# A diffusion block kernel: the first five row blocks of two input projections summed without the token root, the shift added as column sums, modulation products in pairs

## The chip, the core and the metric

The kernel runs on one core of one Trainium2 chip. The core's engines are named as the profile names them: PE (TensorE) multiplies matrices, PEld is its loading of the stationary operand, DVE (VectorE), ACT (ScalarE) and POOL (GpSimd) work elementwise, and SP (SyncE) issues transfers. Sixteen DMA engines move data between HBM and the core's memory; transfers are asked for by SP, ACT and POOL, each through a queue of its own in which requests stand in order. Each engine carries out its instructions in the order of the built program and waits at an instruction until what it needs is there. The metric is the device time of one execution in microseconds (us), as the median of several runs.

## What is computed

A modulation vector made from `c` scales and shifts the normalised tokens; the result `h` goes through one wide input projection, which feeds attention, a Fourier mixer and gates. Cut to what matters here:

```python
shift, scale, gate = jnp.split(silu_c @ w_ada[l] + b_ada[l], 3, axis=-1)
h = _modulate(_rmsnorm(xs, norm_g[l]), shift[:, None], scale[:, None])
p = h @ w_l
...
y_b = (_fourier_mix(u_b) * jax.nn.silu(z_b)) @ w_pb

def _rmsnorm(x, g):
    xf = x.astype(jnp.float32)
    y = xf * lax.rsqrt(jnp.mean(xf * xf, axis=-1, keepdims=True) + EPS)
    return (y * g.astype(jnp.float32)).astype(x.dtype)
def _modulate(h, shift, scale):
    return h * (1 + scale) + shift
```

So for feature d and token t, h = x · rx(t) · gain(d) + shift(d), with gain(d) = norm_g(d) · (1 + scale(d)) and rx(t) the reciprocal root over all 2048 features of the token ("the root" below). There are 512 tokens, 2048 features and 256 context tokens.

## The kernel before

Features lie on the 128 partitions in 16 row blocks `kb` of 128, tokens along the free axis: `xt` is 128 x 16 x 512. The program has a first stage, which this change rewrites, and a long rest (products of `h` with the other weights, attention, branches, output), which it leaves as it is.

The first stage makes three things for each row block and uses them.

*Modulation* (`modulation`, `matvec`, `columns`, L462 and L534 to L591). For block kb the 256 columns of `w_ada` that give its shift and scale are loaded as two tiles `wa` of 1 MB. Sixteen small matmuls (L534, 32 output partitions x 256, in float32, two records each in the trace) multiply them with silu(c). The result is copied by ACT (`ado`, L542), turned by two transposes (L545), reduced by DVE (L551), and two DVE instructions make `shift` (L590) and `gain` (L591) of the block. Four `wa` tiles exist, so the weights of a block are asked for when the product two blocks earlier has ended. Blocks 0 to 2 are loaded through SP's queue, the others through POOL's.

*Rows* (`make_h`, L521 to L523). DVE multiplies `xt` by gain and root, ACT adds the shift and rounds to a high half `hhi`, DVE subtracts for a low half `hlo`. Ahead of the first block stand the token norms (`token_norms`, L482 to L503): all of `xt` is loaded first (L466, six loads), ACT and DVE square it, PE sums the squares over partitions (L497), ACT and DVE make the root (L501, L502), and four matmuls spread it over the partitions (`spread`, L508).

*Sums of u and z* (`start_work`, `mm3`, L328 to L330). Eight tiles of 128 output columns (t 0 to 3 are u, t 4 to 7 are z) are summed over all 16 row blocks, three matmuls for each tile and block (high x high, high x low, low x high), 384 in all, each 128 x 128 on 512 columns. Their weights come as pieces `wr` (L213, up to 512 KB), split into halves `whi` (ACT, L177) and `wlo` (DVE, L178). The u tiles stay in four PSUM banks ("pb" in the profile) through all blocks; z tiles go through two banks ("pc") and `keep` adds each to `part` in SBUF (L562, L564), so the third z tile of a block waits until the first is kept.

The order is left to a scheduler in this stage; the loop over `kb` asks for pieces, splits them (`SPLIT`) and hands out as much of the sums as the finished rows allow. Rows also feed `form_row` (L606 to L608) for later products. After the u sums follows the Fourier mixer: `halves` (L670, L671) makes sums and differences of u on DVE, splits them into `uh` and `ul`, the tables `fch` and `fsq` are split likewise, and PE multiplies (`channels`, then `positions`); the last 48 matmuls of the z sums stand beside this preparation. The first product of the rest (tile "x" in the profile) begins at 169.55 us.

## Time and profile before

| | us |
|---|---|
| median of 3 runs | 1306.72 (1304.67 to 1308.26) |
| the profiled execution, its own time | 1305.55 |
| its span, first to last instruction | 1303.3 |
| PE busy | 1279.5 |
| DVE busy | 995.1 |
| ACT busy | 685.4 |
| DMA moved | 318.54 MB, mean 244 GB/s |

The granted TensorE clock was 0.998 over the span. In the timeline a row gives start, duration, engine, line, operation, output<-input, and in brackets how long the engine had been idle and what ended that. Records of matmuls overlap, so the distance from one start to the next says more than a record's duration. In a row of windows each engine has its busy time and, as (x...), its number of records, then the granted clock, the busy share of the DMA engines and GB/s.

### The profile page before, as it was taken

How to read it: one execution, taken by the hardware profiler on the slowest of the kernel's cores; microseconds unless marked ns; L12 is line 12 of the kernel's file. 1: busy time of each engine (PE TensorE's matmuls, PEld its weight loads, DVE VectorE, ACT ScalarE, POOL GpSimd, SP SyncE). 2: the span in 40 equal slices, each digit the busy share in tenths (PEclk: the TensorE clock that was granted, in tenths of full speed). 3: DMA queues.
4: the chain of work that ended last, by engine and by line, in shares of the span. 5: the costliest groups of instructions: out<-in, count | busy, mean ns of one | idle time of the engine just before them, and what ended most of it. 6: DMA issues, size and time to landing. Idle time of an engine off the chain costs nothing.

```text
span 1303.3 us, 17544 instructions
## 1 busy us (share of the span) xinstructions
PE 1279.5 (98%) x6522; PEld 1047.4 (80%) x6522; DVE 995.1 (76%) x1295; ACT 685.4 (53%) x1079; POOL 180.6 (14%) x244
## 2 busy tenths in 40 slices
PE   6999999999999999999999999999999999999997
PEld 3577888888888888888888888888888888888885
DVE  4666899979688887657687766688798867887676
ACT  5222655555556465444254554666666646464544
POOL 0110011110202111011021010011110212221210
PEclk9999999999999999999999999999999999999999
DMA  9898487887899988976879897468872899998985
GB/s 382 338 373 349 178 244 183 242 243 255 209 284 260 265 287 271 292 209 179 273 200 267 294 224 258 169 221 245 251 230 82 236 246 250 244 212 232 220 205 173
DMA packets 103718, 318.54 MB, mean 244 GB/s; under 512 B 9808, under 2 KB 33104, under 8 KB 99280
## 3 DMA queue, kind: packets, MB, share of 16 engines
q0 software_dynamic: 30288, 123.75, 40.4%
q1 hardware_dynamic: 48720, 163.65, 35.3%
q10 hardware_dynamic: 24624, 30.02, 6.6%
q8 instruction: 51, 0.84, 0.2%
q14 instruction: 35, 0.29, 0.1%
HBM read 283.30 MB, written 34.09 MB: 244 GB/s over the span
## 4 chain that ended last, share of the span: by engine, by line
PE 91%; DMA 3%; DVE 2%; ACT 2%; issue 1%; SPq 0%; ACTq 0%; DVEq 0%
PE banks L328 10%; PE banks L329 10%; PE banks L330 10%; PE x L328 9%; PE x L330 9%; PE x L329 9%; PE y L329 7%; PE y L328 7%; PE y L330 7%; PE pd L534 2%; PE banks L1294 2%; PE pb L328 2%; PE pb L330 2%; PE pb L329 2%; DMA wa<-in_w_ss 1%; PE pc L328 1%
## 5 line engine op out<-in xcount | busy, mean ns | idle before, releaser
L177 ACT ACTIVATE whi<-R 128x1024 fp32r<-128x1024 f32 x138 | 145.2, 1059 | 140.2 <-PE banks L330 47.3
L178 DVE TENSOR_TENSOR wlo<-R,whi 128x1024 fp32r<-128x1024 f32 x138 | 167.5, 1221 | 55.4 <-ACT whi L177 55.2
L178 DVE TENSOR_TENSOR wlo<-wr,whi 128x1024 fp32r<-128x1024 f32 (+1 forms) x123 | 148.5, 1212 | 63.4 <-ACT whi L177 63.2
L177 ACT ACTIVATE whi<-wr 128x1024 fp32r<-128x1024 f32 (+1 forms) x123 | 128.8, 1051 | 116.6 <-PE y L330 37.4
L328 PE MATMUL banks<-whi,s 128*128 128x512 f32 x396 | 157.1, 397 | 2.2 <-DVE ev L862 1.5
L330 PE MATMUL banks<-whi,s 128*128 128x512 f32 x396 | 155.2, 392 | 0.0
L329 PE MATMUL banks<-wlo,s 128*128 128x512 f32 x396 | 155.1, 392 | 0.0
L328 PE MATMUL x<-whi,s 128*128 128x512 f32 x352 | 137.2, 390 | 0.0
L330 PE MATMUL x<-whi,s 128*128 128x512 f32 x352 | 137.0, 389 | 0.0
L329 PE MATMUL x<-wlo,s 128*128 128x512 f32 x352 | 137.0, 389 | 0.0
L328 PE MATMUL y<-whi,s 128*128 128x512 f32 x316 | 123.1, 389 | 0.4 <-DVE cxe L1015 0.4
L329 PE MATMUL y<-wlo,s 128*128 128x512 f32 x316 | 123.1, 390 | 0.3 <-DVE wlo L178 0.3
L330 PE MATMUL y<-whi,s 128*128 128x512 f32 x316 | 122.8, 389 | 0.0
L281 POOL DMA_DIRECT2D R<-in_w_g x64 | 55.9, 874 | 420.2 <-DVE wlo L178 247.5
L177 ACT ACTIVATE s<-wr 128x512 fp32r<-128x512 f32 (+2 forms) x93 | 60.4, 676 | 68.6 <-DMA wr<-cf_d 21.8
L178 DVE TENSOR_TENSOR s<-wr,s 128x512 fp32r<-128x512 f32 (+2 forms) x93 | 66.8, 749 | 31.7 <-ACT s L177 30.9
L328 PEld LDWEIGHTS banks<-whi,s 128*128 128x128 f32 x396 | 74.4, 188 | 17.7 <-ACT whi L177 1.9
L330 PEld LDWEIGHTS banks<-whi,s 128*128 128x128 f32 x396 | 74.4, 188 | 15.5
L329 PEld LDWEIGHTS banks<-wlo,s 128*128 128x128 f32 x396 | 74.4, 188 | 14.0 <-DVE wlo L178 0.2
L330 PEld LDWEIGHTS x<-whi,s 128*128 128x128 f32 x352 | 66.1, 188 | 13.8
L329 PEld LDWEIGHTS x<-wlo,s 128*128 128x128 f32 x352 | 66.1, 188 | 13.6
L328 PEld LDWEIGHTS x<-whi,s 128*128 128x128 f32 x352 | 66.1, 188 | 13.6
(293 smaller groups left out, 2829.4 us busy)
## 6 DMA issues: line engine op xcount, KB each, us to landing
wr<-in_w_g SPq DMA_DIRECT2D x128, 512.0 KB, 5.2
R<-in_w_g POOLq DMA_DIRECT2D x64, 512.0 KB, 7.5
wa<-in_w_ss POOLq DMA_DIRECT2D x26, 1024.0 KB, 8.2
R<-in_w_g SPq DMA_DIRECT2D x32, 512.0 KB, 5.6
wr<-in_w_gate SPq DMA_DIRECT2D x32, 512.0 KB, 5.1
wr<-in_w_o SPq DMA_DIRECT2D x24, 512.0 KB, 7.7
R<-in_w_o POOLq DMA_DIRECT2D x24, 512.0 KB, 9.5
wr<-in_w_pab SPq DMA_DIRECT2D x20, 512.0 KB, 6.4
```

The source lines that it names most:

```text
L177: first = nc.scalar.activation(hi, src, ACT.Copy)
L178: return first, nc.vector.tensor_tensor(lo, src, hi.bitcast(F32), op=ALU.subtract)
L281: nc.gpsimd.dma_start(chain[e.pc], e.nxt, accum_op=ALU.add)
L328: nc.tensor.matmul(o, ah, bh, start=start, stop=False, skip_group_check=cont)
L329: nc.tensor.matmul(o, ah, bl, start=False, stop=False, skip_group_check=cont)
L330: nc.tensor.matmul(o, al, bh, start=False, stop=stop, skip_group_check=cont)
L534: last = nc.tensor.matmul(acc[32 * j : 32 * j + 32, :256], c2[:, 8 * h + k, :], w[:, k, :], start=n < 4, stop=n >= KK - 4)
L1294: nc.tensor.transpose(tp[:, k * P : (k + 1) * P], p[:, k * P : (k + 1) * P], ident)
```

## The change

The sums of u and z over the first five row blocks (`RAWS = 5`) are made from rows without root and without shift: `make_raw` gives ACT x · gain as the high half, and DVE the low half. For these blocks the u tiles are also taken out of PSUM into `part` after block 4. When the root is known, all eight kept sums are multiplied by it (`spread_rows`), and the sums go on with whole rows from block 5. The shift's part of the first five blocks is a product of one column with the weights: `shift_sums` multiplies four 256-column pieces of the raw weights with the block's shift (L574 of the changed file, float32, 32 output partitions), adds the results up over the blocks (`csum`), `shift_columns` turns them, and the last `keep` of each tile adds the column. Rows 0 to 4 are made once more with root and shift, for the later products.

The norms move behind the start: `squares` stands in the loop, DVE adds all 16 squares into one tile one after the other, and one matmul (`norm_sum`) and the spreading stand inside block 4. Loads on SP are put into one order by hand: weights of block 0, the first two blocks of x, pieces, weights of block 1, and so on, x in six chunks between; weights up to block 6 go through SP's queue. PE's order in the stage is written out by hand. From block 10 on the modulations come in pairs ahead of the rows that need them. Matmuls on constants (`warm`) stand ahead of the first modulation (7) and between it and the first sum (5). Modulations use two fixed PSUM tiles (`two`), in the second halves of which the column sums and the turned columns lie. The last pieces of the sums are cut anew: 36 matmuls of z, not 48, stand behind the last u matmul.

```diff
-STEPS = ([(0, 1, 0, 2), (0, 1, 2, 6)] + [(k, 1, 0, 8) for k in range(1, 4)]
-         + [(k, 2, t, 4) for k in range(4, 12, 2) for t in (0, 4)] + [(12, 2, 0, 4), (14, 2, 0, 4)]
-         + [(12, 4, t, 2) for t in (4, 6)])
+RAWS = 5
+STEPS = ([(0, 1, 0, 2), (0, 1, 2, 6)] + [(k, 1, 0, 8) for k in range(1, 6)]
+         + [(k, 2, t, 4) for k in range(6, 12, 2) for t in (0, 4)]
+         + [(12, 2, 0, 4), (12, 2, 4, 2), (14, 2, 0, 4), (14, 2, 4, 2), (12, 4, 6, 2)])
-XCH = [(0, 2), (2, 2), (4, 4), (8, 4), (12, 2), (14, 2)]
+XCH = [(0, 2), (2, 2), (4, 3), (7, 3), (10, 3), (13, 3)]
...
+    wada = {0: wada_load(0)}
+    load_x(0)
+    for _ in range(2):
+        load_start()
+    wada[1] = wada_load(1)
+    load_start()
+    load_x(1)
...
+    def squares(a, n):
+        for q in range(a, a + n):
+            v = sq[q // 2][:, q % 2, :]
+            nc.scalar.activation(v, xt[:, q, :], ACT.Square)
+            if q:
+                nc.vector.tensor_tensor(total, total, v, op=ALU.add)
+    two = [ps.tile([P, 512], F32, tag="b2", bufs=2, name=uid("pd")) for _ in range(2)]
+    cacc, wacc = two[0][:, 256:], two[1][:, 256:]
...
+    def shift_sums(kb):
+        w = [t[:, i : i + 256] for t, n in start_raw.pop(kb) for i in range(0, n, 256)]
+        for j in range(4):
+            nc.tensor.matmul(cacc[32 * j : 32 * j + 32], sf[:, kb, :], w[j], start=True, stop=True)
+        if kb == 0:
+            nc.scalar.copy(csum, cacc)
+        else:
+            nc.vector.tensor_tensor(csum, cacc, csum, op=ALU.add)
...
+    def norm_sum():
+        acc = bank3()
+        norm_acc.append(acc)
+        nc.tensor.matmul(acc, ones, total, start=True, stop=True)
...
+    def make_raw(kb):
+        rows_of(kb)
+        act = nc.scalar.activation(hhi[kb], xt[:, kb, :], ACT.Identity, scale=gain[:, kb, 0:1])
+        return nc.vector.scalar_tensor_tensor(hlo[kb], xt[:, kb, :], gain[:, kb, 0:1], hhi[kb].bitcast(F32),
+                                              op0=ALU.mult, op1=ALU.subtract), act
...
+    def keep(t, acc, kb, nk):
+        dst = pt(t)
+        if kb == 0 or t < 4 and kb < RAWS:
+            nc.scalar.copy(dst, acc)
+        elif kb + nk == KK:
+            nc.vector.scalar_tensor_tensor(dst, acc, corr[:, t : t + 1], dst, op0=ALU.add, op1=ALU.add)
+        else:
+            nc.vector.tensor_tensor(dst, acc, dst, op=ALU.add)
...
+    with tc.manual_schedule(engines={mybir.EngineType.PE}):
+        warm(7)
+        ins = modulate(0)
+        with behind((ins, columns(0))):
+            split_next()
+        warm(5)
+        for kb in range(RAWS):
+            ins = make_raw(kb)
+            with behind(ins):
+                for _ in range(2 if kb == 0 else 1):
+                    split_next()
+                if kb < RAWS - 1:
+                    squares(*XCH[kb])
+                if kb >= RAWS - 2:
+                    squares(*XCH[kb + 1])
...
+            if kb < RAWS - 1:
+                some((5, 3, 3, 3)[kb])
+            else:
+                some(2)
+                norm_sum()
+                some(1)
+            shift_sums(kb)
+            modulate(kb + 1)
+            some(1)
+            columns(kb + 1)
+            if kb == RAWS - 1:
+                act = norm_spread()
+            some(2 if kb == 0 else 4)
+            if kb + 2 <= RAWS:
+                load_start()
+        shift_columns()
...
+        ins = make_h(RAWS)
+        with behind(ins):
+            spread_rows(4, 5)
+            split_next()
...
+        for kb in range(6, KK, 2):
+            ins = make_h(kb), make_h(kb + 1)
...
+                some(8 if kb < KK - 4 else 4)
+                modulate(kb + 2)
+                modulate(kb + 3)
+                some(1 if kb < KK - 4 else 2)
+                columns(kb + 2)
+                columns(kb + 3)
```

`some(n)` is n tiles of the sums, three matmuls each; `modulate` is the product and the copy, `columns` the turning and what follows it.

339 lines of the change are left out of this document (191 added, 148 removed).

## The prediction

> **What bounds the kernel now.** I read the page first: the span, the busy times, the 40 slices, the chain that ended last.
>
> ```profile
> span 1303.3 us, 17544 instructions
> PE 1279.5 (98%) x6522; PEld 1047.4 (80%) x6522; DVE 995.1 (76%) x1295; ACT 685.4 (53%) x1079; POOL 180.6 (14%) x244
> ...
> PE   6999999999999999999999999999999999999997
> ...
> PE 91%; DMA 3%; DVE 2%; ACT 2%; issue 1%; SPq 0%; ACTq 0%; DVEq 0%
> ```
>
> PE is busy for 98% of the span and carries 91% of the chain; only the first of its slices, 32.6 us long, falls under 9. A gain must come from there, or from fewer matmuls. So I read the timeline of the first 30 us.
>
> ```profile
> 1.18 2.98 SPq L466 DMA_DIRECT2D xt<-in_xT  x6
> 4.20 0.95 SPq L462 DMA_DIRECT2D wa<-in_w_ss  x2
> 8.50 8.65 PE L497 MATMUL pd<-s,ones 128*128 128x512 f32 x16 [8.50 <-DVE s L496]
> 18.92 1.07 PE L534 MATMUL pd<-wa,c 128*32 128x256 f32 x16 [0.77 <-DMA wa<-in_w_ss]
> 20.06 0.37 ACT L542 COPY ado<-pd 128x256 f32<-128x256 f32 x1 [0.42 <-PE pd L534]
> 20.82 1.06 PE L508 MATMUL pc<-s 128*128 128x128 f32 x8
> 21.09 0.17 DVE L551 TENSOR_REDUCE adr<-pd 128x4 f32<-128x16 f32 x1 [0.99 <-PE pd L545]
> 21.71 1.46 PE L557 MATMUL pc<-ado,ones 128*128 128x256 f32 x6
> 21.91 0.75 DVE L521 SCALAR_TENSOR_TENSOR xt<-xt,gain,pc 128x512 f32<-128x512 f32 x1 [0.20 <-PE pc L508]
> 22.70 0.72 ACT L522 ACTIVATE s<-xt,shift 128x512 fp32r<-128x512 f32 x1 [0.16 <-DVE xt L521]
> 23.47 1.20 PE L328 MATMUL pb<-s,whi 128*128 128x512 f32 x4 [0.30 <-ACT s L522]
> ```
>
> The first sum starts at 23.47. Ahead of it stand the norms, which need all of x (six loads asked for from 1.18), and behind x in SP's queue the weights of modulation 0, whose second half is awaited until 18.92. From there copy, transposes, spreading of the root, DVE's row and ACT's row take 4.55 us. Then I asked how dense PE is afterwards, in two windows with the matmul groups of each (pb and pc on L328; L329 and L330 have the same counts).
>
> ```profile
> 23.47:63.01 39.54, 38.97 (x270) 23.38 (x271) 23.29 (x42) 10.16 (x17) 5.56 (x10) 1.00 0.91 357
> 63.01:141.27 78.26, 78.22 (x581) 55.64 (x581) 51.31 (x102) 23.92 (x35) 8.61 (x16) 1.00 0.85 330
> ...
> L534 PE MATMUL pd<-wa,c 128*32 128x256 f32 x161 | 12.9, 384 | 0.1
> L328 PE MATMUL pc<-s,whi 128*128 128x512 f32 x16 | 7.1, 446 | 0.1
> L328 PE MATMUL pb<-s,whi 128*128 128x512 f32 x17 | 6.6, 428 | 0.7 <-ACT s L522 0.7
> ...
> L328 PE MATMUL pb<-s,whi 128*128 128x512 f32 x47 | 18.9, 416 | 0.0
> L328 PE MATMUL pc<-s,whi 128*128 128x512 f32 x34 | 14.1, 414 | 0.0
> ```
>
> The chain of waits gives the price of each kind on PE, and one dense run the spacing of the sums.
>
> ```profile
> 62.69 0.23 PE pd L545 x2
> 78.13 1.86 PE pd L534 x32
> 79.99 0.43 PE pb L328
> ...
> 129.74 0.39 PE L328 MATMUL pb<-s,whi 128*128 128x512 f32 x1
> 132.24 0.39 PE L330 MATMUL pb<-s,wlo 128*128 128x512 f32 x1
> ```
>
> From 129.74 to 132.24 are eleven steps: 0.228 us a sum matmul. A modulation costs 1.86, 0.20 more on the matmul behind it (0.43 for 0.23), and 0.23 for its transposes: 2.29. The first window holds 99 sum matmuls and five modulations (161 records, 32 each): 22.6 + 11.4 = 34.0 of 39.54, so 5.5 us of waiting that the idle columns hardly name. The second holds 241 and ten: 54.9 + 22.9 = 77.8 of 78.26, so nothing to gain.
>
> **The start.** The new order loads the weights of modulation 0 first. The first x load (0.55 MB with the vectors) landed 3.9 us after 1.18, and the second half of those weights, 6.05 MB into the queue, at 18.92.
>
> ```profile
> xt<-in_xT SPq DMA_DIRECT2D x1, 512.0 KB, 3.9
> ```
>
> That is 13.8 us for 5.5 MB, 2.5 us a MB. At 2.05 MB the weights land at 5.1 + 3.75 = 8.85, and x at 10.1. From 18.92 to 23.47 were 4.55 us; DVE's multiplication (21.91 to 22.70) goes, so the row could be there at 12.6. But PE must first do five matmuls on constants, in a bank that DVE's reduction reads; it ended 2.34 us after the weights, and three such matmuls took 1.46 us, so five take 2.4: 8.85 + 2.34 + 2.4 = 13.6. Bounds: 12.6 if they cost nothing, 15.3 if PE is slow there (below). I take 13.6, a gain of 9.9.
>
> **Work added to PE behind the start.** Norm and spreading stood ahead of 23.47 and now stand inside block 4. A record of L497 took 0.43 in its dense part, as the weight loads show, and a matmul has two: 0.86, the spreading 1.06 (L508), and 0.20 each on the sum behind it. Shift sums: four matmuls shaped like L534, 8 of 32 records in 1.86, 0.47 a block, 2.3 for five; they stand beside a modulation, with no further change of kind. Turning their sum: 0.23. Modulations in pairs (blocks 10 to 15) save three changes, 0.6. Together +4.2. Bounds 3.6 (the shift sums run beside others at half their price, less the pairs) and 5.4 (each has a change of its own, 5 x 0.2, and pairs save nothing).
>
> ```profile
> 11.22 0.34 PEld L497 LDWEIGHTS pd<-s,ones 128*128 128x128 f32 x1 [0.52 <-DVE s L496]
> 12.27 0.19 PEld L497 LDWEIGHTS pd<-s,ones 128*128 128x128 f32 x1 [0.24 <-DVE s L493]
> 12.70 0.19 PEld L497 LDWEIGHTS pd<-s,ones 128*128 128x128 f32 x1 [0.24 <-issue]
> ```
>
> **Waits in the early blocks.** The order of the changed program is known, only its times are not. These rows carry the prices:
>
> ```profile
> L564 DVE TENSOR_TENSOR part<-pc,part 128x512 f32<-128x512 f32 x31 | 21.1, 686 | 5.0 <-PE pc L330 4.9
> L178 DVE TENSOR_TENSOR wlo<-wr,whi 128x1024 fp32r<-128x1024 f32 x15 | 18.2, 1220 | 1.0 <-ACT whi L177 1.0
> L523 DVE SCALAR_TENSOR_TENSOR s<-xt,shift,s 128x512 fp32r<-128x512 f32 x16 | 12.0, 749 | 3.2 <-ACT s L522 3.2
> L177 ACT ACTIVATE whi<-wr 128x1024 fp32r<-128x1024 f32 x15 | 15.6, 1047 | 1.2 <-DMA wr<-in_w_start 1.2
> ```
>
> I followed the engines block by block. (1) Blocks 0 and 1: the low half of the next row stands on DVE behind three `keep`: 0.4 and 0.9. (2) Modulations 2 and 4 write the PSUM tile whose other half DVE reads for the column sums: PE waits for an addition of 0.42 us (256 wide, as the row at 141.72 below) and in block 3 for the two DVE jobs ahead of it: 0.5 and 0.85. (3) In blocks 2 and 3 `keep` of the first z tile stands behind a weight split that starts after ACT's copy: 0.37 + 1.05 + 1.22 + 0.69 = 3.3 us, and PE has 0.68 + 0.23 + 1.37 = 2.3 us of other work until it needs that bank: 1.05 twice. (4) `norm_sum` waits for the last three of 15 additions in line on DVE, behind a `keep`: 0.69 + 3 x 0.69 less six matmuls, 1.4: 1.5. (5) Behind block 4 the low half of row 5 stands behind four `keep`, 1.05, and the root's copy keeps a bank, 0.5. Sum 7.8 against 5.5 now, so +2.3 if nothing overlaps better than counted, 0 if these waits are like today's, -2.8 if half of them vanish. I take +1.2.
>
> Hidden by DVE's idle time: 15 additions of squares (10.4), column sums (1.7), eight sums times the root (5.5), the low half of five rows a second time (3.7), 21 us in all. The two windows leave DVE idle for 16.25 and 26.95 us. In the early part, though, the additions, the column sums and four of the products, 14.9 us, meet 16.25: nearly full. Transfers: weights of blocks 3 to 6 move from POOL's queue to SP's, behind waits for PE; x and the pieces stand behind them. Weights of block 2 end 8.1 MB into the queue, 24.0 us by the rate above, and PE comes to them at about 25.3; later ones have more room. So loads cost nothing, and each us that they are late by more than 1.3 costs one.
>
> **The end of the stage.** Today ACT copies the u sums; now DVE does it, with the column, ahead of the table splits, and on ACT two splits of weights for the first product stand ahead of `uh`.
>
> ```profile
> 141.72 0.42 DVE L670 TENSOR_TENSOR u<-part 128x256 f32<-128x256 f32 x1
> 143.61 1.17 ACT L177 ACTIVATE uh<-u 128x512 fp32r<-128x512 f32 x2
> 144.12 1.22 DVE L178 TENSOR_TENSOR fsq<-wr,fsq 128x1024 fp32r<-128x1024 f32 x1
> 154.89 0.39 PE L328 MATMUL pb<-fsq,ah 128*128 128x256 f32 x1 [0.26 <-DVE al L178]
> ```
>
> Behind the last u matmul DVE has the last `keep` (0.85 with its handover), two table splits (1.22 each), one of a quarter (0.4) and two half-row jobs (0.7 in a row), then ACT `uh` (0.6): 5.0 us. PE has 12 matmuls, 2.7 us, and then stands before the Fourier matmuls: 2.3. Their low half stands behind two more jobs and a weight split on DVE: another 0.7. That is 3.0, against 0.26 idle ahead of 154.89 today. +2.7 if so, 0 if DVE gets there earlier; I take +1.8, nearer the upper end because the order of DVE is fixed there. The matmuls themselves are the same number. Behind this stage PE's order is the same, and PE was dense there.
>
> **Sum.** -9.9 + 4.2 + 1.2 + 1.8 = -2.7. The profiled execution of 1305.55 (its span 1303.3, and 2.25 around it) would become 1302.9; it stands 1.17 under the median of 1306.72, and from that the forecast is 1304.0.
>
> **Rivals.** *A second path, less waiting:* the early waits shrink to half of the list and the end costs nothing: -9.9 + 4.2 - 1.6 + 0 = -7.3, 1299.4; with today's waits and no cost at the end, -5.7, 1301.0. I give 1300.2. For it: from 63 us on PE never waited with DVE at 51.31 of 78.26. Against it: the program's order names the waits.
>
> *DVE becomes the bound (slower):* blocks 1 to 5, where 14.9 us of new DVE work meet 16.25 idle. If DVE falls behind, each late `keep` holds one of two banks and pushes the next; the list doubles to 15.6, that is 10.1 over today, and the end takes 2.7: -9.9 + 4.2 + 10.1 + 2.7 = +7.1, 1313.8; the middle of this case is 1310. It decides once the waits of these blocks pass 9.4 us (5.5 + 9.9 - 4.2 - 1.8). For it: the share; against it: from 145 to 150 us DVE is full and PE doesn't pause.
>
> ```profile
> 145.00:150.00 5.00, 5.00 (x24) 4.05 (x23) 5.00 (x12) 2.98 (x4) 0.00 (x0) 1.00 0.74 250
> ```
>
> *PE slow at the first sums:* weight loads took 0.34 until 11.22 and 0.19 from 12.27, with PE's first matmul at 8.50, so PE ran at about half rate for some 3.3 us. If the seven early matmuls on constants don't hold, or the holes behind them undo it, half of 3.3 us is lost, 1.7: 1305.7. Today's hole ahead of 18.92 (0.77) undid nothing. The Trainium skill, TensorE: Matmul & The Clock Gate, section "What's actually happening", says that PE's clock is halved by default, is released after about 3.4 us of sustained work and falls back after an idle window of that length; the trace agrees with the release (3.3 us). By that rule holes of 1 to 2 us, as here, would leave the clock up, and the sum stays as it is.
>
> *The change doesn't do what it says:* loads in flight share the engines, so that the first weights land with what was asked for beside them, 5.6 MB in, at 17.7: 22.5 instead of 13.6, +6.2, 1312.9. Against it: x landed piece after piece.
>
> **How the numbers follow.** Forecast 0.38, less waiting 0.32, DVE the bound 0.20, PE slow 0.06, loads together 0.04. About 0.3% (3.9 us) is what a measurement of this kernel can tell from no change: faster means under 1302.8, slower over 1310.6. The forecast's own range, by its bounds, is 1301 to 1307; a quarter of it lies under 1302.8. Faster: 0.10 + 0.31; slower: 0.12 from DVE, 0.03 from the loads; the rest 0.44. The range of 1298 to 1310.5 leaves out the far ends of the second and third case.
>
> **What would show it.** First sum (pb, L328) at 13.6: weights first. Modulation 6 begins with 123 sum matmuls done, by the sum at 13.6 + 28.0 + 5 x 2.29 + 4.8 + 6.7 = 64.6; near 61.8 it is less waiting, from 67.3 on the gain is gone, at 73.5 DVE is the bound. A wait of PE at `norm_sum` of about 1.5 on DVE, waits on pc for `keep`, and about 3 at the Fourier matmuls on ACT's `uh`: the single items. The window from modulation 6 to the last u matmul without waits. The forecast is wrong if the first sum starts after 15.5, or if a wait on a transfer of over 1 us stands between 14 and 66 us, or if PE loses time behind the stage, where its order hasn't changed.

## The result, and the profile after

The changed kernel is slower: 1314.49 us against 1306.12 us in the same comparison (medians of four runs each), a ratio of 1.0064 with a 95% interval of 1.0046 to 1.0081. The forecast was 1304.0 with a range of 1298 to 1310.5; the time lies outside it, on the other side. The profiled execution took 1313.97 us with a span of 1312.2, so 8.9 us of span have to be found. The page first: span, busy times, the slices of PE, the chain that ended last.

```profile
span 1312.2 us, 17694 instructions
PE 1281.3 (98%) x6568; PEld 1051.5 (80%) x6568; DVE 1011.6 (77%) x1328; ACT 691.6 (53%) x1095; POOL 176.3 (13%) x236
...
PE   8899999999999999999999999999999999999997
...
PE 86%; DMA 6%; DVE 5%; ACT 2%; issue 2%; SPq 0%; ACTq 0%; DVEq 0%
```

PE's busy time grew by 1.8 us only, and its share of the chain fell from 91% to 86%: most of the 8.9 must be waiting. In the slices of 33 us, where 699 stood now stands 889: the start is denser, and the second slice is no longer full. The timeline of PE around the first sum shows that the start did what was wanted.

```profile
10.50 0.44 PE L554 MATMUL pd<-ident,ado 128*128 128x128 f32 x2 [0.49 <-ACT ado L550]
11.21 2.43 PE L535 MATMUL pd<-s,ones 128*128 128x256 f32 x10 [0.27 <-DVE adr L560]
13.28 0.59 PE L328 MATMUL pb<-s,whi 128*128 128x512 f32 x1
```

The first sum starts at 13.28, 10.2 us ahead of today's 23.47. The windows behind it (busy time and records of each engine, then granted clock, DMA share, GB/s) show where this goes. The first two are cut where modulation 6 begins (70.10, with 123 sum matmuls done) and behind the last u matmul (146.12, with 348 done).

```profile
13.28:70.10 56.82, 47.94 (x348) 29.91 (x346) 36.64 (x65) 25.72 (x50) 1.26 (x2) 1.00 0.89 357
70.10:146.12 76.02, 74.56 (x567) 53.03 (x567) 59.70 (x123) 26.12 (x40) 8.64 (x16) 1.00 0.82 314
146.10:176.58 30.48, 27.54 (x182) 25.55 (x181) 29.42 (x46) 17.38 (x26) 0.54 (x1) 0.94 0.52 192
```

To modulation 6 the stretch is 17.3 us longer than the 39.54 of before. 24 more sums (123 for 99) are 5.5 of it, so 11.8 are new. The last window runs from 348 sums done to the first x product (176.58; before it is 169.39, not the 169.55 named ahead). The same stretch of the kernel before, where the 349th sum matmul starts at 143.31:

```profile
143.31:169.39 26.08, 25.82 (x182) 24.07 (x180) 25.29 (x38) 15.81 (x26) 0.54 (x1) 1.00 0.62 226
```

That is 4.4 us more. The account of the span: start -10.2, to modulation 6 +11.8, from there to 348 sums +1.2 (76.0 us for 225 sums, before 80.3 for 249, of which the 24 more are 5.5), the end of the stage +4.4, together +7.2 at the first x product; behind it 1135.6 us follow, 1133.9 before, +1.7. Of this, 0.4 stands in the last 10 us and came in every version of the changed kernel; the rest is within what executions differ by: over the profiled executions of this document the same rest took 1133.8 to 1139.9.

The single waits of the early blocks stand in the timeline; in brackets, PE's idle time and what ended it.

```profile
22.69 0.50 PE L329 MATMUL pb<-s,whi 128*128 128x512 f32 x1 [0.29 <-DVE s L611]
25.91 1.93 PE L541 MATMUL pd<-wa,c 128*32 128x256 f32 x32 [0.55 <-DVE csum L578]
28.87 1.06 ACT L177 ACTIVATE whi<-wr 128x1024 fp32r<-128x1024 f32 x1 [4.91 <-DMA wr<-in_w_start]
30.24 0.44 PE L554 MATMUL pd<-ident,ado 128*128 128x128 f32 x2 [1.50 <-ACT ado L550]
34.57 0.50 PE L329 MATMUL pb<-s,whi 128*128 128x512 f32 x1 [0.31 <-DVE s L611]
42.61 0.50 PE L328 MATMUL pc<-s,whi 128*128 128x512 f32 x1 [1.14 <-DVE part L639]
48.00 1.93 PE L541 MATMUL pd<-wa,c 128*32 128x256 f32 x32 [1.14 <-DVE csum L578]
53.50 0.50 PE L328 MATMUL pc<-s,whi 128*128 128x512 f32 x1 [1.08 <-DVE part L639]
58.15 1.13 PE L590 MATMUL pc<-s,ones 128*128 128x512 f32 x2 [1.65 <-DVE s L527]
66.33 0.50 PE L328 MATMUL pc<-s,whi 128*128 128x512 f32 x1 [0.42 <-DVE part L639]
68.62 0.50 PE L328 MATMUL pc<-s,whi 128*128 128x512 f32 x1 [0.41 <-ACT corr L583]
69.43 0.50 PE L329 MATMUL pc<-s,whi 128*128 128x512 f32 x1 [0.31 <-DVE s L620]
74.18 0.50 PE L328 MATMUL pc<-s,whi 128*128 128x512 f32 x1 [1.04 <-DVE part L639]
```

Most items that the prediction listed are there at nearly their size: column sums 0.55 and 1.14 (predicted 0.5 and 0.85), `keep` 1.14 and 1.08 (1.05 twice), `norm_sum` 1.65 (1.5). Smaller were the waits for the low halves of rows 1, 2 and 5: 0.29, 0.31 and 0.31 (0.4, 0.9 and 1.05). Two were not predicted, and in both a late transfer is behind it. ACT's copy of modulation 2 stood behind the split of a piece that landed only at 28.8; so PE, which had the modulation's transposes next, stood 1.50 us until 30.24. And 1.04 at 74.18: pieces asked for too late, as ACT's rows show (ACTq is its queue of requests).

```profile
64.30 0.59 ACT L600 COPY rx<-pc 128x512 f32<-128x512 f32 x1 [0.53 <-PE pc L599]
64.31 3.49 ACTq L213 DMA_DIRECT2D wr<-in_w_start  x2
67.84 0.72 ACT L619 ACTIVATE s<-xt,shift 128x512 fp32r<-128x512 f32 x1 [2.96 <-DVE part L639]
...
71.20 1.06 ACT L177 ACTIVATE whi<-wr 128x1024 fp32r<-128x1024 f32 x1 [2.58 <-DMA wr<-in_w_start]
```

The requests stand behind `rx` in ACT's order; they took 3.5 us, until 67.80, and ACT's row of block 5 came right behind them. (The profile names a DVE job as what ended that wait, but the DVE job that makes the row's input, L618, had ended at 65.67.)

At the end of the stage stands the wait that the prediction named, and DVE's line-up ahead of it: the last four `keep` of u, which ACT made before, two table splits, one quarter split, four sums and differences.

```profile
144.74 2.72 DVE L637 SCALAR_TENSOR_TENSOR part<-pb,corr,part 128x512 f32<-128x512 f32 x4
147.38 2.35 DVE L178 TENSOR_TENSOR fsq<-wr,fsq 128x1024 fp32r<-128x1024 f32 x2
149.65 0.41 DVE L178 TENSOR_TENSOR fch<-wr,fch 128x256 fp32r<-128x256 f32 x1
149.98 0.42 DVE L812 TENSOR_TENSOR u<-part 128x256 f32<-128x256 f32 x1
...
151.76 0.38 PE L328 MATMUL pb<-fch,uh 128*128 128x256 f32 x1 [2.77 <-ACT uh L177]
```

Behind the wait of 2.77 us the granted clock fell to half for one stretch of 3.4 us, as PE's windows show.

```profile
149.86:153.26 3.40, 1.33 (x9) 1.00 1.02 405
153.26:156.66 3.40, 3.40 (x16) 0.50 1.01 413
```

### The profile page after: what moved, and what is told of

The parts are those of the page before. It is cut to its first block, busy times and chain, and to the rows that moved or that the text cites. A ratio compares the mean times of both kernels' runs of the same rounds, so it can differ in the third digit from the quotient of the medians.

```text
span 1312.2 us, 17694 instructions
## 1 busy us (share of the span) xinstructions
PE 1281.3 (98%) x6568; PEld 1051.5 (80%) x6568; DVE 1011.6 (77%) x1328; ACT 691.6 (53%) x1095; POOL 176.3 (13%) x236
## 4 chain that ended last, share of the span: by engine, by line
PE 86%; DMA 6%; DVE 5%; ACT 2%; issue 2%; SPq 0%; ACTq 0%; DVEq 0%
PE banks L328 10%; PE banks L329 10%; PE banks L330 10%; PE x L330 8%; PE x L329 8%; PE x L328 8%; PE y L329 7%; PE y L328 7%; PE y L330 7%; DMA wr<-in_w_start 2%; PE banks L1436 2%; PE pd L541 1%; DMA wa<-in_w_ss 1%; DVE wlo L178 1%; PE pb L330 1%
## 5 line engine op out<-in xcount | busy, mean ns | idle before, releaser
L178 DVE TENSOR_TENSOR wlo<-wr,whi 128x1024 fp32r<-128x1024 f32 (+2 forms) x124 | 148.4, 1204 | 73.7 <-ACT whi L177 73.7
L177 ACT ACTIVATE whi<-wr 128x1024 fp32r<-128x1024 f32 (+2 forms) x124 | 128.7, 1044 | 130.9 <-PE banks L330 34.5
L330 PEld LDWEIGHTS x<-whi,s 128*128 128x128 f32 x352 | 66.1, 188 | 13.7
L328 PEld LDWEIGHTS x<-whi,s 128*128 128x128 f32 x352 | 66.1, 188 | 13.7
L329 PEld LDWEIGHTS x<-wlo,s 128*128 128x128 f32 x352 | 66.1, 188 | 13.6
```

The costliest lines, as they stand in the source:

```text
L177: first = nc.scalar.activation(hi, src, ACT.Copy)
L178: return first, nc.vector.tensor_tensor(lo, src, hi.bitcast(F32), op=ALU.subtract)
L328: nc.tensor.matmul(o, ah, bh, start=start, stop=False, skip_group_check=cont)
L329: nc.tensor.matmul(o, ah, bl, start=False, stop=False, skip_group_check=cont)
L330: nc.tensor.matmul(o, al, bh, start=False, stop=stop, skip_group_check=cont)
```

## The experiments

My theory A at the start: the loss is a handful of single waits, each made by one job that stands in a wrong place on DVE or ACT; each can be cured by a change of place. Rival B: DVE has too much to do in the early blocks and at the end; a cure in one place brings the wait back at the next. "x0" below is the start of the first x product in the profile: 169.4 before, 176.6 after. The ratios are to the kernel before, in the same comparison; those of single cures overlap with that of the changed kernel, so there the traces carry the reading. x0 is read from one execution: four executions whose code is the same that far had 348 sums done at 146.1 to 148.9, so 2 us of x0 alone show little. So "the end" is given too, the length of the stretch from 348 sums done to x0, in which the edits at the end of the stage act: 26.1 before, 30.5 after.

**The Fourier wait by order alone.** The sine tables are split behind the first half of u.

```diff
-    for q in range(2):
-        split_from(get(("dfts", q))..., fsq[:, 0, q], fsq[:, 1, q])
+    raws = [get(("dfts", q))... for q in range(2)]
     raw = get(("dftc", 0))
     split_from(raw, fch[:, 0, :], fch[:, 1, :])
-    for g in range(4):
-        halves(g)
+    halves(0)
+    halves(1)
+    for q in range(2):
+        split_from(raws[q], fsq[:, 0, q], fsq[:, 1, q])
+    for g in range(2, 4):
+        halves(g)
```

> The changed kernel with one thing moved: on DVE the table fch and the sums and differences of the first two u tiles stand ahead of the splits of the large table fsq (two of 1.22 us), and on ACT uh stands ahead of the second split of weights R. Theory A (the wait of 2.77 us ahead of the Fourier matmuls comes from what stands ahead of uh on DVE, and the granted clock of 0.5 behind it from the wait): the wait falls under 1 us, the clock stays at 1.0 up to 157 us, the 24 Fourier matmuls take about 3 us in place of 4.96, and the time falls by 3 to 5 us, to about 1310.5. Rival B (the first wait is only moved: ul, later splits or the loads of R take its place, and DVE is the bound in this stretch): under 1.5 us of gain, a wait of 1.5 us or more somewhere between 148 and 165 us.

Measured: 1317.83 us, ratio 1.0082 (1.0069 to 1.0095), x0 at 182.0, of which 2.8 us were lost ahead of the edit (348 sums were done at 148.9, against 146.1; behind a wait at 74.86 the clock fell). The end took 33.1 us, 2.6 more than in the changed kernel. The wait ahead of the Fourier matmuls was gone and a longer one stood behind them, where the z sums need a bank that DVE's `keep` (L637) frees:

```profile
159.76 0.79 PE L328 MATMUL pc<-s,whi 128*128 128x512 f32 x1 [3.90 <-DVE part L637]
```

B is right at the end of the stage. The windows above say why: there DVE is busy for 25.29 of 26.08 us in the kernel before and for 29.42 of 30.48 in the changed one. DVE has 4.1 us more to do in the stretch, and the stretch is 4.4 longer. It had hardly any reserve in the first place.

**The clock at the Fourier matmuls.** Twelve matmuls on constants fill the wait, so that PE does not pause.

```diff
             acc = bank()
+            for _ in range(12 if (g, m2) == (0, 0) else 0):
+                nc.tensor.matmul(acc[:, :P], ones, ones, start=True, stop=True)
```

> The changed kernel with 12 matmuls on constants (ones by ones, 128 columns, float32) in the wait ahead of the Fourier matmuls; nothing else is moved. They add no result. Theory A (PE's pause sets the clock back): the pause on PE shrinks to under 0.6 us, the granted clock stays at 1.0 between 153 and 157 us, the 24 Fourier matmuls take 3 to 3.3 us in place of 4.96 and the time falls by 1.5 to 2 us, to about 1312.7, although uh comes no earlier. Rival B (these matmuls are paced by ul and by the splits of ah, not by the clock): the 24 matmuls still take close to 5 us and the time stays at 1314.5 or rises by up to 0.5.

Measured: 1315.73 us, ratio 1.0074 (1.0059 to 1.0090), x0 at 176.9. The clock stayed at 1.00; 348 sums were done 1.2 us later than in the changed kernel, ahead of the edit, and the end took 29.6 us in place of 30.5. DVE was still the bound there: from 149.86 to 156.66 it was busy without a gap, and the z sums waited 0.42 for its `keep` at 156.94. Two versions below in which nothing is changed at the end and the clock happened to stay up (the column sums in the free tile, the additions on POOL) took 29.6 and 29.7 as well, with waits of 2.44 and 2.46 ahead of the Fourier matmuls. So the half clock at this place explains at most 0.8 of the 4.4 us.

**The column sums in the tile that is free.** They take the half of the PSUM tile that the next modulation does not write.

```diff
-    cacc, wacc = two[0][:, 256:], two[1][:, 256:]
+    wacc = two[1][:, 256:]
...
-        sp = two[kb % 2 if kb > 7 else 1][:, 256:]
+        sp = two[kb % 2][:, 256:]
...
+        cacc = two[kb % 2][:, 256:]
```

> The changed kernel with the column sums of each block put into the PSUM tile that the next modulation does not use. Theory A (the waits of PE ahead of modulations 2 and 4, 0.73 and 1.32 us, are those for DVE's addition in the other half of the same tile): both vanish; the first gives way to the wait on the copy of modulation 2, which stands behind a load, so 1.3 to 2 us are gained, time 1312.5 to 1313.2. Rival B (DVE is the bound in blocks 1 to 5): other waits of PE in 13 to 70 us grow by as much, and the time stays within 0.5 us of 1314.5.

Measured: 1315.42 us, ratio 1.0074 (1.0062 to 1.0086), x0 at 177.5. Both waits on `csum` went, and two on other jobs of DVE came: 1.84 on `keep` at 31.45 and 1.79 on a low half-row at 45.32, each with the half clock behind it. The scheduler had also changed DVE's order with the tile, so this run doesn't separate place from amount.

**Pieces asked for earlier, on SP.**

```diff
             if kb + 2 <= RAWS:
                 load_start()
+            if kb == RAWS - 2:
+                load_start()
+            if kb == RAWS - 1:
+                load_start()
         shift_columns()
         asks[0] = nc.scalar
-        ask_more(act, 2)
```

> The changed kernel with the next two pieces of weights asked for on SP's queue inside blocks 3 and 4, where ACT asked for them behind the copy of the spread root (64.3 us). Theory A (the transfers stood still between 56 and 62 us because nothing was asked for; the wait of 1.04 us at 74.18 on keep comes from the piece that landed late at 71.2, and row 5 on ACT stood 3 us behind its own requests at 64.3): the waits at 68.6 to 69.4 (0.7) and 74.18 (1.04) vanish, 1.2 to 2.2 us are gained, time about 1312.8. Rival B (DVE's additions are what PE waits for there, whatever the loads do): the wait at 74 stays over 0.8 us and the gain is under 0.6.

Measured: 1312.01 us, ratio 1.0047 (1.0035 to 1.0059), x0 at 174.7. The waits at 68.62, 69.43 and 74.18 were gone; modulation 6 began at 68.8 (70.1), and 348 sums were done at 144.3 (146.1). The late request cost about 2 us.

**Twelve of the fifteen additions of squares left out** (only squares 1, 8 and 15 are added to the first; the root is then that of four rows' squares).

```diff
-            if q:
+            if q in (1, 8, 15):
                 nc.vector.tensor_tensor(total, total, v, op=ALU.add)
```

> The changed kernel without 12 of the 15 additions of squares on DVE (8.3 us of its work between 14 and 58 us; the root is then made from four rows' squares only). DVE's other work keeps its order. Theory A (the waits of blocks 1 to 4 come from where a job stands in DVE's and ACT's order): the wait at norm_sum (1.65) and that of modulation 4 on the column sums (1.14), which stand behind such additions, go; the two of 1.14 and 1.08 on keep, which stand behind a weight split, and the one of 1.5 on the copy of modulation 2 stay. Gain 2.3 to 3 us, time 1311.5 to 1312.2. Rival B (DVE's amount of work is the bound in blocks 1 to 4): the keep waits shrink too, gain 5 us or more, under 1309.5.

Measured: 1312.86 us, ratio 1.0049 (1.0031 to 1.0067), x0 at 175.4; modulation 6 at 67.38, 2.7 earlier. DVE lost 12 jobs of 0.69, 8.3 us. `norm_sum` no longer waited; behind a wait at 72.10 the clock fell and took part of the gain again. The second `csum` wait halved to 0.55, but the waits for `keep` stayed as they were:

```profile
42.08 0.50 PE L328 MATMUL pc<-s,whi 128*128 128x512 f32 x1 [1.14 <-DVE part L639]
46.88 1.93 PE L541 MATMUL pd<-wa,c 128*32 128x256 f32 x32 [0.55 <-DVE csum L578]
52.38 0.50 PE L328 MATMUL pc<-s,whi 128*128 128x512 f32 x1 [1.06 <-DVE part L639]
```

So the two waits for `keep` don't come from the amount of work on DVE but from the job that stands ahead of the `keep`, the weight split behind ACT's copy. For them A is right; taking 8.3 us of work from DVE won 2.7 of the 8.8 us that PE waited up to modulation 6.

**The additions of squares on POOL.**

```diff
-                nc.vector.tensor_tensor(total, total, v, op=ALU.add)
+                nc.gpsimd.tensor_tensor(total, total, v, op=ALU.add)
```

> The changed kernel with the 15 additions of squares on POOL in place of DVE; the output is the reference's. Theory A: POOL is idle until 61.74 us and keeps up with the loads of x, so the same two waits go as without the additions, 2.3 to 3 us, time 1311.5 to 1312.2. Rival B (POOL takes over 2 us for an addition, or slows DVE's jobs down while both run): norm_sum waits for POOL longer than 1.65 us and nothing is gained, 1314 or more.

Measured: 1312.23 us, ratio 1.0048 (1.0032 to 1.0064), x0 at 174.9. It did about half of what leaving them out did: modulation 6 at 68.57, 1.5 earlier, the `keep` waits unchanged (1.14 and 1.05); `norm_sum` still waited 0.94, now for POOL, whose additions took 1.37 us in the mean, against 0.69 on DVE.

**The sine tables' low halves on POOL.**

```diff
-        split_from(get(("dfts", q))..., fsq[:, 0, q], fsq[:, 1, q])
+        raw = get(("dfts", q))...
+        nc.scalar.activation(fsq[:, 0, q], raw, ACT.Copy)
+        nc.gpsimd.tensor_tensor(fsq[:, 1, q], raw, fsq[:, 0, q].bitcast(F32), op=ALU.subtract)
```

> The changed kernel with the low halves of the table fsq (two of 1.22 us on DVE, ahead of u) made on POOL. Nothing is put later on DVE for it, unlike the version that only moved them behind u, which then waited 3.9 us for a keep of z. Theory A (the end of the stage is bound by the sum of DVE's work, which grew by the four keeps of u, 2.72 us): the wait ahead of the Fourier matmuls falls under 0.7 us and no wait over 1 us follows before 165 us, gain 2.4 to 4.5 us, time 1310 to 1312. Rival B (positions wait for POOL, or the loads of R bound the end): a wait over 2 us between 148 and 170 us, time 1313.5 or more.

Measured: 1312.28 us, ratio 1.0043 (1.0030 to 1.0056), x0 at 174.9. The Fourier wait was gone and no other over 0.5 us stood at the end, which took 28.1 us: 2.4 less where work left DVE, and 2.6 more where it only moved on DVE (the first run).

**Both: earlier pieces and tables on POOL.**

> The two edits that take a cause away without moving another job: the next two pieces asked for on SP inside blocks 3 and 4 (by itself 2.4 us), and fsq's low halves on POOL. Theory A (two separate places on PE's path): the gains add up, 1307.5 to 1309.5. Rival B (what the one frees the other was waiting for as well): not under 1311.

Measured: 1310.79 us, ratio 1.0027 (1.0012 to 1.0042), x0 at 171.9. 348 sums were done at 143.9, 2.3 us earlier than in the changed kernel (1.8 with the earlier pieces alone), and the end took 28.1, as with the tables on POOL alone: the two gains, in different stretches, add, though the time stayed 1.3 us above theory A's range.

**A new order of the early blocks, with the additions on POOL.** The split of block 1 stands behind modulation 2; ACT's copies of modulations 3 and 4 come right behind the first half of the piece; `keep` comes behind the column's reduction; the last squares stand in block 3.

```diff
-                for _ in range(2 if kb == 0 else 1):
+                for _ in range((2, 0, 1, 1, 1)[kb]):
                     split_next()
...
-                if kb >= RAWS - 2:
-                    squares(*XCH[kb + 1])
+            copied = last_split[-1] if kb in (2, 3) else ()
...
+            if kb == RAWS - 2:
+                squares(*XCH[kb + 1])
+                squares(*XCH[kb + 2])
...
-            modulate(kb + 1)
+            with behind(list(copied[:1]) + (last_sq if kb == RAWS - 2 else [])):
+                ins = modulate(kb + 1)
             some(1)
-            columns(kb + 1)
+            with behind(copied[1:]):
+                keep_after[:] = [columns(kb + 1)]
...
+            if kb == 1:
+                some(2)
+                low_after.append(kept_by[-2])
+                with behind((ins,)):
+                    split_next()
+                low_after.clear()
```

> The version with the additions of squares on POOL, and in it only the order of jobs on ACT and DVE changed in blocks 1 to 4: the copy of modulation 2 ahead of the split that waits for its load; the splits of blocks 2 and 3 ahead of the copies of modulations 3 and 4, in DVE's idle time, and so ahead of the keeps; the squares of the last three rows ahead of the copy of modulation 4. Amount of work and PE's order are the same. Theory A (the keep waits of 1.14 and 1.05, the copy's 0.95 and POOL's 0.94 at norm_sum are a matter of order): all four fall under 0.5, modulation 6 begins with 123 sums done 2.5 to 3.5 us earlier than the 68.57 of the other version, time 1308.5 to 1310. Rival B (DVE or the loads are the bound there): the waits only move, modulation 6 begins after 67.5.

Measured: 1311.44 us, ratio 1.0040 (1.0027 to 1.0053), x0 at 174.6. Against the version with the additions on POOL alone the waits of blocks 1 and 2 fell (0.77 for 0.95; none for the 1.14 at 42), but in block 3 one of 2.52 came on `keep` at 52.97, where the squares now stood ahead of the copy. Modulation 6 began at 67.70, 0.9 earlier. Partly cured, partly moved.

**All cures together:** this order, earlier pieces, the tables on POOL and the column sums in the free half.

> All edits together: two pieces asked for earlier, squares added and fsq's low halves made on POOL, the order of jobs, and the column sums in the tile that the next modulation doesn't use. Theory A: modulation 6 begins at 64 to 65.5 and the first product x at 165.5 to 168 (before: 169.39), without a pause of PE over 1 us from 14 to 165 us and without a lowered clock there; time 1302 to 1304.5, 2 to 4 us under the kernel before. Rival B (the loads, 24 MB at 2.5 us a MB, become the bound of the first 65 us): waits on transfers of 1 us and more appear, x not before 169, time 1305.5 or more.

Measured: 1306.99 us against 1306.21, ratio 1.0004 (0.9996 to 1.0013), x0 at 169.3, where the kernel before has 169.4. The whole loss is back, without the gain of 2 to 4 us that theory A expected. The two longest waits left are in block 3; the third row shows ACT's squares, ahead of the copy that the first one waits for, standing for a chunk of x:

```profile
48.70 0.44 PE L559 MATMUL pd<-ident,ado 128*128 128x128 f32 x2 [1.77 <-ACT ado L555]
52.62 0.50 PE L333 MATMUL pc<-s,whi 128*128 128x512 f32 x1 [2.08 <-DVE part L646]
43.56 1.68 ACT L530 ACTIVATE s<-xt 128x512 f32<-128x512 f32 x3 [1.90 <-DMA xt<-in_xT]
```

Transfers are full in these blocks: in the changed kernel the DMA engines were busy from 14 to 56 us at a share of 1.01, with 413 GB/s (before: 0.95, 376). So beside DVE's and ACT's order the arrival of x and of the pieces sets some of the early waits too.

**Without the five matmuls on constants ahead of the first sum** (`warm(5)` taken out of the last version).

> The version of all edits without the five matmuls on constants between the first modulation and the first sum. Theory A (they are on the path, and the clock would hold without them since PE has worked from 2.2 us on): the first sum starts 0.9 to 1.3 us earlier, at 12.1 to 12.5, the clock stays at 1.0, and the time falls by 0.5 to 1.2. Rival B (the pause that they fill sets the clock back): the clock shows 0.5 for some 3.4 us after 13 us, and the time rises by 0.5 to 1.5.

Measured: 1308.10 us, ratio 1.0012 (1.0004 to 1.0021), x0 at 170.4. The first sum came at 12.14, 0.5 us earlier than in the version with them (12.64), behind a pause of 1.42; then the clock fell to half for a stretch of 3.4 us. Windows of PE:

```profile
8.64:12.04 3.40, 1.51 (x18) 1.00 1.05 425
12.04:15.44 3.40, 3.30 (x7) 0.50 0.99 412
```

What the first sum wins without these matmuls is lost again behind it: they seem worth what they cost, though the two times differ by less than their intervals tell apart. (Later in this execution, at 53, the clock fell once more, so x0 is not a pure measure of this part.)

**The norm behind modulation 5,** with the last squares behind the copy of modulation 4 again and modulation 6 ahead of the first sums of block 5, on top of all cures. The main lines of the edit:

```diff
             if kb == RAWS - 2:
                 squares(*XCH[kb + 1])
-                squares(*XCH[kb + 2])
...
+            if kb == RAWS - 2:
+                with behind((ins,)):
+                    squares(*XCH[kb + 2])
+            if kb == RAWS - 1:
+                norm_sum()
```

> The version of all edits with three more, at the two pauses that its trace still shows (1.77 and 2.08 us in block 3, and the chain of the root): in block 3 the copy of modulation 4 stands ahead of the squares of the last three rows again; norm_sum stands behind modulation 5 and uses a bank of u that is copied out, its spreading stands behind two z tiles; modulation 6 stands ahead of the first sums of block 5 and covers the way from the root to row 5. Theory A (order alone makes the pauses, and PE has the work to fill them): no pause over 1 us between 14 and 165 us, the clock stays at 1.0 there, x begins at 164 to 166.5 (before: 169.39), and the time is 1301 to 1304.5. Rival B (the loads or POOL's additions, 1.3 to 1.5 us each, are the bound up to block 5): a wait of 1 us or more on a transfer or on POOL between 50 and 70 us, x not before 168, time 1305 or more.

Measured: 1307.22 us against 1306.77, ratio 1.0004 (0.9993 to 1.0016), x0 at 170.1. The two waits above shrank to 1.01 and 0.65, but the Fourier wait was back with 2.35 and the clock at half behind it. 348 sums were done at 140.6, 2.7 us ahead of the kernel before, and the end took 29.6; so the gain that theory A expected stayed out. On DVE a job of 0.41 had become one of 2.57 beside POOL's split of the tables:

```profile
139.41 4.75 POOL L840 TENSOR_TENSOR fsq<-wr,fsq 128x1024 fp32r<-128x1024 f32 x2 [22.88 <-PE pb L335]
...
141.88 2.57 DVE L181 TENSOR_TENSOR fch<-wr,fch 128x256 fp32r<-128x256 f32 x1
```

**The four `keep` of u taken from DVE.** The u sums stay in PSUM through all blocks; DVE multiplies them there by the root, and ACT takes the finished sums out with the shift as a bias.

```diff
-        if kb == 0 or t < 4 and kb < RAWS:
+        if kb == 0:
             nc.scalar.copy(dst, acc)
+        elif t < 4:
+            nc.scalar.activation(dst, acc, ACT.Identity, bias=corr[:, t : t + 1])
...
+        for i, acc in enumerate(sums_u):
+            scaled = nc.vector.tensor_tensor(acc, acc, rx, op=ALU.mult)
```

> The changed kernel without the copies of u out of PSUM behind block 4: DVE multiplies the four u banks by the root where they lie (four jobs of about 0.7 us, in place of four on part), PE goes on adding to them from block 5 (u ahead of z there), and ACT copies the final sums with the column as bias, so that DVE has no keep of u left at the end. POOL is not used. Theory A (these four keeps, 2.72 us, are what DVE lacks at the end of the stage): no wait over 1 us ahead of the Fourier matmuls and none between 143 and 165 us, the clock stays at 1.0 there, from the last u matmul to the first product x it takes 23 to 26.5 us as in the kernel before (30.5 in the changed one), and the time falls by 4 to 6 us, to 1308.5 to 1310.5. Rival B (the tables' splits, the loads of R or ACT, which now has the copies, set the end): the wait of 2 us and more stays, time 1312.5 or more. Rival C (block 5 waits for the four products in PSUM): a wait of 1.5 us and more near 68 us, which takes back half of it.

Measured: 1311.06 us, ratio 1.0025 (1.0009 to 1.0042), x0 at 172.7 with the waits of blocks 1 to 4 hardly changed. In place of the Fourier wait of 2.77 us one of 1.33 stands later, at 158.24, and the clock stayed at 1.00. The end took 27.1 us: the four jobs taken from DVE give 3.4 us there, a little less than theory A expected.

**Three more mixtures,** of this part with the new early order: the norm behind modulation 5, the additions on POOL; the same with the additions on DVE; and all cures but the tables on POOL, with this part in their place.

> The last version with the edits of the early blocks: two pieces asked for earlier, squares on POOL, the order of jobs on ACT and DVE, the column sums in the other tile, norm_sum behind modulation 5 and the spreading behind modulation 6; fsq stays on DVE. Theory A (early and late loss are separate and add up): x begins at 164.5 to 167 (before: 169.39), no wait over 1.2 us from 14 to 165 us, time 1302 to 1304.5. Rival B (loads, POOL or DVE bound what is left): x not before 168.5, time 1305.5 or more.

> The same with the additions of squares on DVE as in the changed kernel. Theory A (DVE has room for them once they stand behind the jobs that PE waits for): within 1 us of the version with POOL. Rival B (DVE is full in blocks 2 to 4): keeps or rows of these blocks wait 1 us longer in sum over two blocks, and the time is 1 to 3 us above it.

> The kernel e12_all with one part changed: the split of the sine constants is back on DVE, and u's sums stay in their four banks, where DVE multiplies them by rx and ACT copies the finished sums out with the shift as a bias (as in e15_upsum); so POOL has no 4.75 us of work beside DVE there. Theory A: the two cures add, because one shortens the early waits (e12_all: first x product at 169.3) and the other takes four keeps from DVE ahead of the Fourier matmuls without a job of POOL beside DVE; the first x product at 166 to 169, no wait above 1.3 at the Fourier matmuls, the granted clock at 1.0 there, and a time of 1303 to 1306, at or below before's. Rival B: the multiplications by rx in PSUM stand ahead of rows 5 and 6 on DVE, between rx and the modulations of x; then a wait of 1.5 to 2.5 comes around 68 to 80 on s or xt of rows 5 to 7, the clock falls behind it, and the first x product comes at 170 to 173 with 1307 to 1310.

Measured: 1310.19 us (1.0038, 1.0024 to 1.0051), x0 172.6; 1315.14 us (1.0059, 1.0045 to 1.0073), x0 175.5; 1310.82 us (1.0036, 1.0022 to 1.0049), x0 172.5. None reached the version with all cures, nor the times that their theories A expected. The first two had a wait of 2.29 on the row of block 6 (at 77.44 and 80.66), behind DVE's products in PSUM. The third lost 2.31 on `keep` at 53.03, with the clock at half behind it, and 1.27 at 68.9 for a product in PSUM. Between the first and the second the additions alone differ: on DVE they cost 2.8 us at x0, and the wait for a low half-row in block 3 grew from 0.63 to 1.86, with the clock at half behind it. So in this order DVE's amount of work does count in the early blocks, and B is right there in part.

## Why the prediction was wrong, step by step

*The start: right.* 13.28 for 13.6, a gain of 10.2 for 9.9; leaving out the five matmuls on constants brought it 0.5 us forward and won nothing.

*Work added to PE: right.* Five shift sums at 0.45 are 2.25, norm 0.96, spreading 0.91, turning 0.3: 4.4 in the first window, for 4.8 predicted there.

*Waits in the early blocks: this step failed.* The list came to 7.8, and the waits that answer to it measured 7.3 as idle times of PE. But the prediction set 5.5 us of "waiting" in the kernel before against it, as if the new waits would replace the old. The timeline of before shows that most of the 5.5 was no wait: the scheduler had cut the five modulations in eleven pieces.

```profile
25.28 1.07 PE L534 MATMUL pd<-wa,c 128*32 128x256 f32 x16
26.28 0.50 PE L330 MATMUL pb<-s,wlo 128*128 128x512 f32 x1
...
27.66 1.07 PE L534 MATMUL pd<-wa,c 128*32 128x256 f32 x16
28.66 0.50 PE L328 MATMUL pc<-s,whi 128*128 128x512 f32 x1
...
40.60 0.60 PE L534 MATMUL pd<-wa,c 128*32 128x256 f32 x2
41.14 0.50 PE L328 MATMUL pc<-s,whi 128*128 128x512 f32 x1
42.03 1.93 PE L534 MATMUL pd<-wa,c 128*32 128x256 f32 x30
43.89 0.50 PE L328 MATMUL pb<-s,whi 128*128 128x512 f32 x1
```

From start to next row the eleven take 11.8 us together, each costs 0.2 at its ends, and the transposes add 1.15: 15.1, not 11.4. So 3.7 of the 5.5 are cuts and only 1.8 waits. In the changed kernel the modulations are whole, which really saves 3.7, and against that stand waits of 56.82 - 28.0 - 11.45 - 4.4 = 13.0: the listed ones 7.3, the wait on ACT's copy 1.5, and some 4 that don't show as idle time. Most of these 4 stand around the waits: at the wait of 1.14 the next start is 1.30 late and the row behind takes 0.11 more, by which eleven waits come to 3.0 (an estimate). By the prediction's own accounting 6.7 became 13.0: not +1.2 but +7.5, about the whole list. This is the largest error, some 6 us. That the cuts cost this is read from the timeline; no run has the kernel before with whole modulations.

*"So loads cost nothing": wrong.* It counted bytes up to the weights of block 2 (24.0; they landed at 25.6) and left out the chunk of x and the piece that stand behind them in the queue, and who asks: 1.50 behind that piece, which landed at 28.8, and about 2 us by the late requests on ACT, by the run that asked earlier. The prediction's own sign for this, a wait on a transfer of over 1 us before 66, has no such row on PE; it was ACT that waited, and PE waited for ACT.

*The end: mis-sized.* The wait itself was 2.77, as worked out (3.0); the prediction booked 1.8 and the stretch cost 4.4. The reason is in the row that was quoted against DVE as the bound: "from 145 to 150 us DVE is full and PE doesn't pause". A full engine is one without reserve. Of the four `keep` 1.3 us reach into the stretch, and a table split (1.1) and four sums and differences of u (1.3), which formerly stood ahead of it, came in too; that came straight out as time. In every version the end is within 1.1 us of DVE's busy time in it, except where its jobs were only moved:

| from 348 sums done to x0, us | length | DVE busy |
|---|---|---|
| kernel before | 26.1 | 25.3 |
| changed kernel | 30.5 | 29.4 |
| tables split behind half of u | 33.1 | 30.4 |
| constants in PE's wait | 29.6 | 29.3 |
| tables on POOL | 28.1 | 27.7 |
| four `keep` of u taken from DVE | 27.1 | 26.2 |

*The rivals.* "DVE becomes the bound" was given 0.20, with 1313.8 as its far end. The time is near this end, but by another sum: it placed the bound in blocks 1 to 5, where DVE was busy for 36.64 of 56.82 us and leaving 8.3 us of work out won 2.7; it is the bound at the end of the stage. "PE slow" had the right mechanism at the wrong place: not at the first sum but behind later pauses, and at the Fourier matmuls it cost at most 0.8 us. "Loads together" didn't occur (first weights used at 8.94). "Less waiting" was the farthest off.

*Modulation 6 to the last u matmul* was to be without waits and had the one of 1.04 at 74.18; the stretch cost 1.2 us, and of the 0.6 that the paired modulations were to save nothing shows in it.

*What the change can give.* In the version with all cures the stage is as long as before: the first sum comes 10.8 us earlier, 8.7 are lost again up to modulation 6 (4.4 of PE's time is added work there) and 2.0 at the end. No version tried was faster than the kernel before. Open is whether an order exists in which block 3 doesn't wait without POOL beside DVE, with transfers as full as they are, and where the 0.4 us at the very end come from.

## What to carry to other kernels

Before a list of new waits is set against old ones, take the old ones from the timeline: a stretch that takes longer than its counted work may be made of dearer work, not of waits, and then nothing is there to replace. An engine that is full for a stretch while the bounding engine just keeps up is the next bound; here jobs that came into such a stretch cost about their own duration, taking jobs off the engine helped, and the one new order tried there did not. When all work starts earlier, look at everything that stands in the queue ahead of a transfer, at which engine asks for it and at what that engine waits for.

## What was not expected of the hardware

*The clock falls after far shorter pauses than 3.4 us.* The Trainium skill, TensorE: Matmul & The Clock Gate, section "What's actually happening", puts the fall behind an idle window of about 3.4 us and says that the windows run freely. The runs agree with windows that stand on a grid: in each execution all changes of the granted clock lie whole multiples of 3.41 us apart. They don't agree with idle: a window in which PE is busy for less than about half of its time is enough. In the run with the moved column sums two stretches at half clock began 13.7 us apart, four windows, each behind a window with 1.56 and 1.61 us of work of 3.40 (the second is shown); two windows on the same grid with 1.77, one of them in front of its Fourier matmuls, were without effect. In the first stage of all the runs, with windows laid on each execution's own grid, the clock fell or stayed down behind every one with up to 1.63 us of work; of those with 1.75 to 2.0 only two were followed by a fall (1.81 and 1.96), so the bound is not sharp.

```profile
43.20:46.60 3.40, 1.61 (x8) 1.00 1.02 421
46.60:50.00 3.40, 3.40 (x24) 0.50 1.00 407
```

```profile
148.98:152.39 3.41, 1.77 (x8) 1.00 1.02 406
152.39:155.80 3.41, 2.28 (x15) 1.00 1.02 382
```

So whether a pause of 1.4 to 2.5 us lowers the clock hangs on where it lies in the grid: 2.08 in the version with all cures had no effect, 1.42 in the one without early matmuls had.

*A short job on DVE is held up beside POOL.* 0.41 became 2.57 us while POOL subtracted two tables (4.75 for two); in the four other runs with these tables on POOL the same two took POOL 10.1 us beside other jobs of DVE. The Trainium skill, SBUF — State Buffer, section "Who interferes with whom", says that the two engines share a pair of ports under an exclusive lock, and that a DVE instruction with two inputs from SBUF meets it; the trace agrees, with 2.2 us lost by one short job. Work moved to POOL is therefore not free for DVE.
